# Multiplying the loaded gates two blocks at a time, one pair every second block

## The chip, the cores and the metric

The kernel runs on one NeuronCore of a Trainium2 chip. The metric is the device time of one execution in microseconds (us). TensorE is called PE here, VectorE DVE, ScalarE ACT, GpSimd POOL and SyncE SP; SPq and POOLq are the queues on which SP and POOL issue DMA.

## The reference, cut to what matters

The program is two transformer blocks on 256 tokens of width 2048. The change lies in the last part, a mixture of 16384 tiny experts ("PEER"):

```python
vals, ci = lax.top_k(cand, PEER_TOPK)          # 16 experts for each token and head
g = jax.nn.softmax(vals, axis=-1)              # their gates
...
u = u_table[it]
a = jnp.einsum('td,tkd->tk', ht, u)
w = jax.nn.gelu(a, approximate=False) * gt     # gt: the gates
return jnp.einsum('tk,tkd->td', w, v_table[it])
```

The kernel computes it densely: gelu of all 16384 expert activations, times a gate matrix G that is zero where a token did not choose the expert, times the whole table v.

## The kernel before, in words

The 16384 experts are 128 blocks of 128. Blocks 0 to 63 have their activations in the tile `bigA` ([128, 64, 256], one plane of 128 experts x 256 tokens for each block), blocks 64 to 127 in `bigB`.

- **Stage u** computes the activations, block by block (`u_block`): two weight chunks of 512 KB, 32 matmuls (L367, L370), then ACT copies one half of the result (L425), DVE adds the other (L427), and ACT takes the gelu (L1430). While blocks 0 to 63 run, DVE also selects the experts, and POOL scatters the gates to the matrices G0 and G1 in DRAM, one for each half of the tokens (L1412).
- **Stage v** multiplies with the table v, in four parts of 64 blocks: bigA for the first half of the output columns, bigA for the second, bigB for the second, bigB for the first. A block is one weight chunk of 512 KB and 12 matmuls (L1494 to L1496, four times), and `operands` prepares it.

Every weight chunk comes by DMA into one of 4 `raw` buffers. ACT rounds it to `wh` (L341, 3 buffers) and DVE forms the rest `wl` = raw - wh (L342, 2 buffers). So the `wl` of a chunk can be written only when PE is done with the chunk two before it, and PE's second matmul of a block needs it. The activations are split in the same way: ACT writes the rounded part into `xh` (L1487), DVE the rest (L1488), in a ring of 8 slots (`wxs`). That ring takes the memory of the input of stage u, so nothing is written to it before the last matmul of stage u.

The gate of a block must be multiplied into its plane before the block is split. Gates are loaded in pairs of blocks: `pair` is a [128, 2, 256] tile with 3 buffers, filled by two DMAs of POOL, from G0 and from G1 (L1472). `operands` asks for the pair of its block and the one after, and multiplies plane by plane on DVE (L1486).

A scheduler orders the instructions of each engine ahead of time; an engine then runs its list in order and stands at an instruction whose wait is not fulfilled. `tc.high_priority()` lets the weight splits pass other work. `tc.issue_after(x)` puts an instruction behind x in the list of its engine, and beyond that the scheduler is free. `self.added` is the last addition L427 that was written.

Of the kernel before, what the change touches and what calls it, by code (L numbers as in the profile page):

```python
# [11 lines left out]
F32 = mybir.dt.float32  # L12
# [4 lines left out]
OP = mybir.AluOpType  # L17
# [4 lines left out]
T = 256  # L22
# [164 lines left out]
class K:  # L187
# [871 lines left out]
    def block2(self):  # L1059
# [3 lines left out]
        with ExitStack() as cx:  # L1063
# [190 lines left out]
            TT, STT, TS = nc.vector.tensor_tensor, nc.vector.scalar_tensor_tensor, nc.vector.tensor_scalar  # L1254
            G, G2, GB, _, B, B2 = [ws[:, i:i + 1] for i in range(6)]
            with tc.issue_after(last.ins):
# [15 lines left out]
            TT(a, a, r, OP.mult)  # L1272
            TS(a, a, B, 1.0 / D, op0=OP.add, op1=OP.mult)
            TT(e, e, r, OP.mult)
# [36 lines left out]
    def peer(self, out):  # L1311
        nc, tc, a = self.nc, self.tc, self.a
        W = self.W
        xh = self.h2h
        with ExitStack() as cx:
# [3 lines left out]
            A = bigp.tile([128, 64, T], F32, name="bigA")  # L1319
# [15 lines left out]
            for g in range(4):  # L1335
                q = tk.tile([128, 4, T], F32, name="q", bufs=2)
# [89 lines left out]
            def u_block(b, dst):  # L1426
                def ev(ps):
                    t = self.tmp()
                    self.addh(t.unsqueeze(1), ps)
                    nc.scalar.activation(dst, t, AF.Gelu)  # L1430
                self.dense_t([a["u"][b, c] for c in range(2)], xh, ev, nt=1, kc=8, nw=128)
# [6 lines left out]
            tkc.close()  # L1438
            bigq = cx.enter_context(tc.tile_pool(name="bigB", bufs=1))
            B = bigq.tile([128, 64, T], F32, name="bigB")  # L1440
            for b in range(64):
                u_block(64 + b, B[:, b])
            self.drain()

            def final_rows(row, xs, xt, gt):
# [16 lines left out]
            acc = self.xhp.tile([128, 4, 1024], F32, name="xh")  # L1462
            wxs = self.xhp.tile([128, 8, 512], F32R, name="xh")

            pairs = {}

            def gates(q):

                if q < 64 and q not in pairs:
                    t = pairs[q] = sm.tile([128, 2, T], F32, name="pair", bufs=3)  # L1470
                    for tt in range(2):
                        nc.gpsimd.dma_start(t[:, :, tt * 128:tt * 128 + 128],  # L1472
                                            self.G[tt][:, q * 256:q * 256 + 256].rearrange("p (i t) -> p i t", i=2))
                return pairs.get(q)

            gated = set()

            def operands(big, dh, b):
                H, L = self.wchunk(self.vchunk(dh, b), 1, 1024)
                wx = wxs[:, b % 8]  # L1480
                if b not in gated:
                    gated.add(b)
                    g = gates(b // 2)
                    gates(b // 2 + 1)
                    with tc.issue_after(self.added.ins):
                        nc.vector.tensor_tensor(big[:, b % 64], big[:, b % 64], g[:, b % 2], OP.mult)  # L1486
                nc.scalar.copy(wx[:, :T], big[:, b % 64])  # L1487
                nc.vector.tensor_tensor(wx[:, T:], big[:, b % 64], wx[:, :T].bitcast(F32), OP.subtract)  # L1488
                return H, L, wx

            def product(o, tt, dc, ops, first, last):
# [8 lines left out]
            def part(ps, big, dh, b0, b1, first=False, last=False):  # L1500
                for b in range(b0, b1):
                    ops = operands(big, dh, b)
                    for tt, dc in four:
                        product(ps[tt][dc], tt, dc, ops, first and b == b0, last and b == b1 - 1)
                    self.pump()

            def banks():
                return [[self.bank() for dc in range(2)] for tt in range(2)]
# [30 lines left out]
            def first_half():  # L1539
                for tt, dc in four:  # L1540
                    add(tt, 0, dc, acc[:, tt, dc * 512:dc * 512 + 512])
                    yield

            self.tasks.append(final_rows(row, xs, xt, gt))
            self.tasks.append(first_half())
            part(ps, B, 1, 64, 128, False, True)
            self.drain()
# [3 lines left out]
            ps = banks()  # L1551
            part(ps, B, 0, 64, 125, True)
            ops = [operands(B, 0, b) for b in range(125, 128)]
            for tt in range(2):
                for dc in range(2):
# [47 lines left out]
```

## Time and profile before

| | |
|---|---|
| median of 3 runs | 3229.49 us (3226.41 to 3237.59) |
| the profiled execution | 3225.47 us, span of its trace 3223.7 us |
| PE busy | 3118.0 us (97% of the span) |
| DVE busy | 2381.3 us (74%) |
| ACT busy | 1738.8 us (54%) |
| POOL busy | 665.1 us (21%) |

Busy time is an average over the whole program. PE is close to full, so what there is to win are the stretches in which it stands or runs slowly, and these are read from the rows below, stage by stage. Stage u ends at about 2461 us of the span, stage v is the rest.

### The profile page before, as it was taken

What the parts mean: (1) busy time and instruction counts of PE and PEld (TensorE: products, weight loads), DVE (VectorE), ACT (ScalarE), POOL (GpSimd) and SP (SyncE); (2) the same over time, 40 slices, a digit from 0 to 9 for tenths busy, and PEclk for the clock granted to TensorE, in tenths of its full rate; (3) what the DMA queues carried; (4) which work ended last, traced back from release to release, by engine and by line L of the source; (5) the groups of instructions that cost most, each with busy time, mean ns of one, the idle gap of its engine ahead of it and who ended that gap; (6) DMA issues with size and microseconds to landing.
All of it is one profiled execution on the core that took longest, in us unless ns stands there. A gap on an engine that the chain in (4) does not pass through costs nothing.

```text
span 3223.7 us, 45942 instructions
## 1 busy us (share of the span) xinstructions
PE 3118.0 (97%) x16626; PEld 2671.7 (83%) x16626; DVE 2381.3 (74%) x3945; ACT 1738.8 (54%) x2632; POOL 665.1 (21%) x429
## 2 busy tenths in 40 slices
PE   8999899999999998999989999999999899999997
PEld 7888788888888887888878888888887678888886
DVE  6768889889999998668879985555556765555656
ACT  6676654444444576556665665455554345455453
POOL 0000000000000001000005778877862610000000
PEclk9999999999999998999989999999999999999999
DMA  6655589999999848555446776677676766565554
GB/s 236 206 177 185 170 280 328 331 335 325 330 327 332 304 162 333 177 174 166 148 146 164 183 184 190 190 190 190 190 201 215 253 210 194 192 228 196 191 194 150
DMA packets 235316, 715.55 MB, mean 222 GB/s; under 512 B 60512, under 2 KB 60896, under 8 KB 234448
## 3 DMA queue, kind: packets, MB, share of 16 engines
q1 hardware_dynamic: 185472, 671.97, 61.2%
q0 software_dynamic: 48176, 35.74, 6.4%
q10 hardware_dynamic: 1440, 4.91, 0.4%
q8 instruction: 130, 2.13, 0.3%
q14 instruction: 98, 0.80, 0.1%
HBM read 690.22 MB, written 21.11 MB: 221 GB/s over the span
## 4 chain that ended last, share of the span: by engine, by line
PE 78%; DVE 9%; DMA 2%; issue 1%; ACT 1%; POOL 0%; DVEq 0%; POOLq 0%; ACTq 0%
PE bank L367 37%; PE bank L370 19%; PE bank L1495 6%; PE bank L1494 6%; PE bank L1496 6%; DVE wl L342 3%; DMA pair<-G 2%; PE bank L412 1%; PE bank L413 1%; PE bank L414 1%; POOL pair L1472 0%; DVE t L1307 0%; PE bank L629 0%; ACT wh L341 0%; DVE sel L1378 0%
## 5 line engine op out<-in xcount | busy, mean ns | idle before, releaser
L342 DVE TENSOR_TENSOR wl<-raw,wh 128x1024 fp32r<-128x1024 f32 x1066 | 1302.1, 1222 | 717.4 <-PE bank L370 355.7
L367 PE MATMUL bank<-xh,wh 128*128 128x512 f32 x5264 | 1729.0, 396 | 37.3 <-DVE xh L455 20.5
L341 ACT CAST wh<-raw 128x1024 fp32r<-128x1024 f32 x1067 | 1119.2, 1050 | 846.3 <-PE bank L367 695.2
L370 PE MATMUL bank<-xh,wl 128*128 128x256 f32 x5264 | 1297.0, 282 | 0.3
L367 PEld LDWEIGHTS bank<-xh,wh 128*128 128x128 f32 x5264 | 980.1, 189 | 248.4 <-issue 19.4
L370 PEld LDWEIGHTS bank<-xh,wl 128*128 128x128 f32 x5264 | 930.9, 190 | 23.3 <-DVE wl L342 6.6
L1412 POOL DMA_INDIRECT G<-gate,at x256 | 550.3, 2150 | 183.6 <-DMA G<-gate,at 96.9
L1495 PE MATMUL bank<-wl,xh 128*128 128x512 f32 x1016 | 400.7, 394 | 24.7 <-DVE wl L342 24.5
L1494 PE MATMUL bank<-wh,xh 128*128 128x512 f32 x1020 | 400.8, 393 | 2.6 <-ACT xh L1487 2.6
L1496 PE MATMUL bank<-wh,xh 128*128 128x512 f32 x1020 | 399.5, 392 | 0.0
L1495 PEld LDWEIGHTS bank<-wl,xh 128*128 128x128 f32 x1016 | 192.2, 189 | 74.4 <-DVE wl L342 35.5
L1067 POOL DMA_DIRECT2D masks<-masks x1 | 0.7, 698 | 1218.6 <-DVE acc_z L472 1218.6
L771 DVE CUSTOM_DVE_ANT_0 raw<-raw,crow 128x1024 f32<-128x1024 f32 x192 | 234.0, 1219 | 15.4 <-DMA raw<-w_ada 15.3
L1494 PEld LDWEIGHTS bank<-wh,xh 128*128 128x128 f32 x1020 | 192.9, 189 | 43.4 <-ACT xh L1487 2.9
L1496 PEld LDWEIGHTS bank<-wh,xh 128*128 128x128 f32 x1020 | 193.0, 189 | 39.7
L367 PE MATMUL bank<-fx,wh 128*128 128x512 f32 x704 | 180.6, 393 | 0.0
L427 DVE TENSOR_TENSOR tmp<-bank,tmp 128x256 f32<-128x256 f32 x388 | 153.5, 419 | 11.0 <-ACT tmp L425 10.2
L1487 ACT CAST xh<-bigA 128x256 fp32r<-128x256 f32 x128 | 51.9, 408 | 198.2 <-PE bank L1495 194.3
L367 PEld LDWEIGHTS bank<-fx,wh 128*128 128x128 f32 x704 | 126.9, 189 | 23.4 <-DVE fx L903 0.2
L1487 ACT CAST xh<-bigB 128x256 fp32r<-128x256 f32 x128 | 52.3, 409 | 173.6 <-PE bank L1495 173.6
L425 ACT COPY tmp<-bank 128x256 f32<-128x256 f32 x388 | 132.1, 373 | 22.9 <-PE bank L370 22.2
L1472 POOL DMA_DIRECT2D pair<-G x128 | 91.2, 720 | 107.6 <-DVE bigA L1486 81.0
(405 smaller groups left out, 2353.7 us busy)
## 6 DMA issues: line engine op xcount, KB each, us to landing
raw<-u SPq DMA_DIRECT2D x256, 512.0 KB
raw<-v SPq DMA_DIRECT2D x256, 512.0 KB
raw<-w_ada SPq DMA_DIRECT2D x192, 512.0 KB
raw<-w_gu SPq DMA_DIRECT2D x176, 512.0 KB
raw<-w_in SPq DMA_DIRECT2D x144, 512.0 KB
raw<-w_down SPq DMA_DIRECT2D x88, 512.0 KB
raw<-w_out SPq DMA_DIRECT2D x32, 512.0 KB
raw<-w_ple_gate SPq DMA_DIRECT2D x32, 512.0 KB
```

The source lines that it names most:

```text
L341: nc.scalar.copy(H[:, :n], raw[:, :n])
L342: nc.vector.tensor_tensor(L[:, :n], raw[:, :n], H[:, :n].bitcast(F32), OP.subtract)
L367: self.nc.tensor.matmul(p, lhsT=H[:, kk, c], rhs=xh(k0 + kk), start=k0 + kk == 0, stop=False)
L370: self.nc.tensor.matmul(p[:, T:], lhsT=L[:, kk, c], rhs=xh(k0 + kk)[:, :T], start=False, stop=k0 + kk == nk - 1)
L425: self.nc.scalar.copy(out[:, j], p[:, T:])
L427: self.added = self.nc.vector.tensor_tensor(out[:, j], p[:, :T], out[:, j], OP.add)
L771: nc.vector.tensor_tensor_reduce(raw, raw, self.crow[:, h * 1024:h * 1024 + 1024], 1.0, 0.0, OP.mult, OP.add, s[:, h:h + 1])
L1412: nc.gpsimd.indirect_dma_start(out=self.G[tt].rearrange("p (f o) -> (p f) o", o=1), out_offset=bass.IndirectOffsetOnAxis(ap=places[tt, h][ ...
L1487: nc.scalar.copy(wx[:, :T], big[:, b % 64])
L1494: nc.tensor.matmul(o, lhsT=wH, rhs=H[:, 0, c], start=first, stop=False)
L1495: nc.tensor.matmul(o, lhsT=wH, rhs=L[:, 0, c], start=False, stop=False)
L1496: return nc.tensor.matmul(o, lhsT=wL, rhs=H[:, 0, c], start=False, stop=last)
```

## The change: what it does

The pairs are now numbered in the order of the blocks, P0 to P63, and two helpers work through them. `load_gates` starts the two DMAs of the next pair, and `apply_gates` starts one more load and multiplies the oldest loaded pair into its two planes, in one instruction of 128x512. It is called after each of the last five blocks of stage u (P0 to P4) and then in every second block of stage v, five pairs ahead of its use, so that P63 is multiplied in block 116 of the 256. In stage v `self.added` is now the split L1488 of the block just written, and so the multiplication stands behind that split in DVE's list; in stage u it is still the addition of the block.

```diff
+            loaded = deque()
+            blocks = deque(range(0, 128, 2))
+            def load_gates():
+                if blocks:
+                    b = blocks.popleft()
+                    t = sm.tile([128, 2, T], F32, name="pair", bufs=3)
+                    for tt in range(2):
+                        nc.gpsimd.dma_start(t[:, :, tt * 128:tt * 128 + 128],
+                                            self.G[tt][:, b * 128:b * 128 + 256].rearrange("p (i t) -> p i t", i=2))
+                    loaded.append((b, t))
+            def apply_gates():
+                load_gates()
+                if loaded:
+                    b, t = loaded.popleft()
+                    w = (A if b < 64 else B)[:, b % 64:b % 64 + 2]
+                    with tc.issue_after(self.added.ins):
+                        nc.vector.tensor_tensor(w, w, t, OP.mult)
             for b in range(64):
                 u_block(64 + b, B[:, b])
+                if b == 57:
+                    load_gates()
+                    load_gates()
+                if b >= 59:
+                    apply_gates()
...
             def operands(big, dh, b):
                 H, L = self.wchunk(self.vchunk(dh, b), 1, 1024)
                 wx = wxs[:, b % 8]
-                if b not in gated:
-                    gated.add(b)
-                    g = gates(b // 2)
-                    gates(b // 2 + 1)
-                    with tc.issue_after(self.added.ins):
-                        nc.vector.tensor_tensor(big[:, b % 64], big[:, b % 64], g[:, b % 2], OP.mult)
                 nc.scalar.copy(wx[:, :T], big[:, b % 64])
-                nc.vector.tensor_tensor(wx[:, T:], big[:, b % 64], wx[:, :T].bitcast(F32), OP.subtract)
+                self.added = nc.vector.tensor_tensor(wx[:, T:], big[:, b % 64], wx[:, :T].bitcast(F32), OP.subtract)
+                if b % 2 == 0:
+                    apply_gates()
                 return H, L, wx
```

How the lists move is shown at three places of DVE. Two are at the hand-over from stage u to stage v. Line numbers after the changed lines shift: L1486 (multiplication) becomes L1461, L1488 (split) L1496, L1472 (gate load) L1450. V0, V1, ... are the blocks of stage v.

DVE before, at the hand-over: `wl_23746` belongs to V1, `wl_23768` to V2, and the addition of `tmp_23787` is the last one of stage u.

```order
L427 TENSOR_TENSOR tmp_23738<-bank_23693,tmp_23738 128x256
L342 TENSOR_TENSOR wl_23719<-raw_23716,wh_23718 128x1024
L342 TENSOR_TENSOR wl_23746<-raw_23743,wh_23745 128x1024
L427 TENSOR_TENSOR tmp_23787<-bank_23742,tmp_23787 128x256
L1486 TENSOR_TENSOR bigA_15923<-bigA_15923,pair_23803 128x256 x2
L1486 TENSOR_TENSOR bigA_15923<-bigA_15923,pair_23806 128x256
L1488 TENSOR_TENSOR xh_23792<-bigA_15923,xh_23792 128x256 x3
L1486 TENSOR_TENSOR bigA_15923<-bigA_15923,pair_23806 128x256
L1486 TENSOR_TENSOR bigA_15923<-bigA_15923,pair_23851 128x256 x2
L1488 TENSOR_TENSOR xh_23792<-bigA_15923,xh_23792 128x256 x2
L342 TENSOR_TENSOR wl_23768<-raw_23765,wh_23767 128x1024
L1488 TENSOR_TENSOR xh_23792<-bigA_15923,xh_23792 128x256
```

DVE now, at the same place: `pair_23654` is P3, `pair_23760` P5, `pair_23813` P6, `pair_23707` P4; `wl_23737`, `wl_23768` and `wl_23790` belong to V0, V1 and V2, and `tmp_23809` is the last addition of stage u.

```order
L427 TENSOR_TENSOR tmp_23756<-bank_23711,tmp_23756 128x256
L1461 TENSOR_TENSOR bigA_15923<-bigA_15923,pair_23654 128x512
L342 TENSOR_TENSOR wl_23737<-raw_23734,wh_23736 128x1024
L1496 TENSOR_TENSOR xh_23818<-bigA_15923,xh_23818 128x256
L1461 TENSOR_TENSOR bigA_15923<-bigA_15923,pair_23760 128x512
L1496 TENSOR_TENSOR xh_23818<-bigA_15923,xh_23818 128x256 x2
L342 TENSOR_TENSOR wl_23768<-raw_23765,wh_23767 128x1024
L1461 TENSOR_TENSOR bigA_15923<-bigA_15923,pair_23813 128x512
L427 TENSOR_TENSOR tmp_23809<-bank_23764,tmp_23809 128x256
L1461 TENSOR_TENSOR bigA_15923<-bigA_15923,pair_23707 128x512
L342 TENSOR_TENSOR wl_23790<-raw_23787,wh_23789 128x1024
```

The first split of V0 no longer stands behind the last addition of stage u, multiplications have moved ahead into stage u, and P4 now comes behind P5, P6 and that last addition.

The rows right behind these, now: `pair_23831` is P7, `pair_23875` P8, and `wl_23826` and `wl_23850` belong to V3 and V4.

```order
L1496 TENSOR_TENSOR xh_23818<-bigA_15923,xh_23818 128x256 x2
L1461 TENSOR_TENSOR bigA_15923<-bigA_15923,pair_23831 128x512
L1496 TENSOR_TENSOR xh_23818<-bigA_15923,xh_23818 128x256
L342 TENSOR_TENSOR wl_23826<-raw_23823,wh_23825 128x1024
L1496 TENSOR_TENSOR xh_23818<-bigA_15923,xh_23818 128x256
L1461 TENSOR_TENSOR bigA_15923<-bigA_15923,pair_23875 128x512
L1496 TENSOR_TENSOR xh_23818<-bigA_15923,xh_23818 128x256 x2
L342 TENSOR_TENSOR wl_23850<-raw_23847,wh_23849 128x1024
```

Each of these `wl` stands behind the multiplication of another pair than before. With 3 buffers, P7 is loaded into the buffer that P4 leaves.

Further into stage v, DVE before has three or four multiplications for every block:

```order
L342 TENSOR_TENSOR wl_23917<-raw_23914,wh_23916 128x1024
L1488 TENSOR_TENSOR xh_23792<-bigA_15923,xh_23792 128x256
L1486 TENSOR_TENSOR bigA_15923<-bigA_15923,pair_24301 128x256
L1486 TENSOR_TENSOR bigA_15923<-bigA_15923,pair_24346 128x256 x2
L342 TENSOR_TENSOR wl_23938<-raw_23935,wh_23937 128x1024
L1488 TENSOR_TENSOR xh_23792<-bigA_15923,xh_23792 128x256
L1486 TENSOR_TENSOR bigA_15923<-bigA_15923,pair_24391 128x256 x2
L1486 TENSOR_TENSOR bigA_15923<-bigA_15923,pair_24436 128x256 x2
```

DVE now, further into stage v:

```order
L1496 TENSOR_TENSOR xh_23818<-bigA_15923,xh_23818 128x256
L1461 TENSOR_TENSOR bigA_15923<-bigA_15923,pair_24007 128x512
L342 TENSOR_TENSOR wl_23914<-raw_23911,wh_23913 128x1024
L1496 TENSOR_TENSOR xh_23818<-bigA_15923,xh_23818 128x256
L342 TENSOR_TENSOR wl_23938<-raw_23935,wh_23937 128x1024
L1496 TENSOR_TENSOR xh_23818<-bigA_15923,xh_23818 128x256
```

One multiplication stands in the list for every two blocks, behind a split, and this pattern lasts until P63.

## Rows read from the trace of the kernel before

**Rows 1.** Stretches: length, busy PE, PEld, DVE, ACT, POOL; granted clock, DMA share, GB/s.

```profile
2300.00:2400.00 100.00, 100.00 (x579) 88.17 (x578) 51.69 (x54) 50.30 (x72) 79.31 (x37) 1.00 0.71 194
2463.00:2605.00 142.00, 116.36 (x454) 87.60 (x455) 102.96 (x210) 53.59 (x83) 86.37 (x122) 0.95 0.78 249
2605.00:2825.00 220.00, 219.92 (x971) 181.78 (x970) 127.67 (x164) 112.04 (x166) 0.00 (x0) 1.00 0.60 195
```

**Rows 2.** Waits from 2461 to 2606 us: total, times, longest.

```profile
PE bank L1495 <- DVE wl L342: 24.5, 21, 2.4
...
DVE bigB L1486 <- DMA pair<-G: 22.1, 16, 2.5
DVE bigA L1486 <- DMA pair<-G: 16.6, 19, 1.8
...
PE bank L1494 <- ACT xh L1487: 2.6, 1, 2.6
```

**Rows 3.** PE in order of time: the end of stage u, the start of stage v.

```profile
2461.22 0.28 PE L370 MATMUL bank<-xh,wl 128*128 128x256 f32 x1
2464.06 0.50 PE L1494 MATMUL bank<-wh,xh 128*128 128x512 f32 x1 [2.56 <-ACT xh L1487]
```

**Rows 4.** DVE in order of time, just after the last gate multiplication.

```profile
2608.72 1.23 DVE L342 TENSOR_TENSOR wl<-raw,wh 128x1024 fp32r<-128x1024 f32 x1 [0.90 <-issue]
```

**Rows 5.** Groups of DVE from 2458.7 to 2608 us.

```profile
L342 DVE TENSOR_TENSOR wl<-raw,wh 128x1024 fp32r<-128x1024 f32 x40 | 48.8, 1219 | 2.7 <-PE bank L370 2.7
L1486 DVE TENSOR_TENSOR bigB<-bigB,pair 128x256 f32<-128x256 f32 x64 | 24.6, 421 | 22.2 <-DMA pair<-G 22.1
L1486 DVE TENSOR_TENSOR bigA<-bigA,pair 128x256 f32<-128x256 f32 x64 | 24.6, 421 | 16.8 <-DMA pair<-G 16.6
```

**Rows 6.** The nearest group to a multiplication of 128x512 on DVE.

```profile
L1534 DVE TENSOR_TENSOR bigA<-bigA,xh 128x512 f32<-128x512 f32 x12 | 8.2, 680 | 0.1
```

**Rows 7.** DVE in order of time, the last blocks of stage u.

```profile
2457.27 0.42 DVE L427 TENSOR_TENSOR tmp<-bank,tmp 128x256 f32<-128x256 f32 x1
2458.77 1.23 DVE L342 TENSOR_TENSOR wl<-raw,wh 128x1024 fp32r<-128x1024 f32 x1 [1.07 <-PE bank L370]
2461.60 1.23 DVE L342 TENSOR_TENSOR wl<-raw,wh 128x1024 fp32r<-128x1024 f32 x1 [1.60 <-PE bank L370]
```

**Rows 8.** One block of stage v without gates, all engines in order of time.

```profile
2654.90 0.41 ACT L1487 CAST xh<-bigA 128x256 fp32r<-128x256 f32 x1 [1.36 <-PE bank L1495]
2654.93 0.39 PE L1494 MATMUL bank<-wh,xh 128*128 128x512 f32 x1
...
2654.96 1.23 DVE L342 TENSOR_TENSOR wl<-raw,wh 128x1024 fp32r<-128x1024 f32 x1 [1.16 <-issue]
...
2656.10 0.42 DVE L1488 TENSOR_TENSOR xh<-bigA,xh 128x256 fp32r<-128x256 f32 x1
...
2657.65 0.39 PE L1494 MATMUL bank<-wh,xh 128*128 128x512 f32 x1
...
2657.88 0.39 PE L1495 MATMUL bank<-wl,xh 128*128 128x512 f32 x1
```

**Rows 9.** The chain that ended last, from a freed gate buffer to its load landed.

```profile
2478.07 0.28 issue
2478.36 0.71 POOL pair L1472
2479.07 4.56 DMA pair<-G
...
2506.34 0.28 issue
...
2508.74 5.46 DMA pair<-G
```

**Rows 10.** Size of a gate load, two of which make a pair.

```profile
pair<-G POOLq DMA_DIRECT2D x128, 128.0 KB
```

**Rows 11.** A stretch with one fall of the granted clock, columns as in Rows 1.

```profile
2500.00:2520.00 20.00, 15.38 (x57) 11.62 (x58) 13.94 (x28) 6.35 (x9) 12.18 (x18) 0.91 0.79 251
```

More of the change, by code (lines that the diff above doesn't have):

```diff
@@ L1463, in peer @@
             wxs = self.xhp.tile([128, 8, 512], F32R, name="xh")
[L1465 to L1476, printed above, removed]
             def operands(big, dh, b):
```

## The prediction

> **What bounds the kernel now.** I read the busy time by stretches first. In stage u (2300 to 2400 us) and in the later stage v (2605 to 2825) PE is busy all the time at clock 1.00, and nothing can be won there. In between, from 2463 to 2605 us, PE is busy for 116 of 142 us at a mean clock of 0.95, while DVE is busy for 103 us and POOL issues gate loads [rows 1]. The view of the waits says who holds whom: PE waits 24.5 us for `wl` from DVE, and DVE stands 22.1 + 16.6 = 38.7 us for gate loads to land [rows 2]. So this stretch is paced by the gate loads: all 128 multiplications are in it [rows 5], DVE stands in front of them, and the `wl` behind them in its list come late to PE. Ahead of it PE stands once for 2.56 us, until the first block of stage v is multiplied and split [rows 3].
>
> What the stretch costs is counted in blocks. Undisturbed, a block of stage v takes 2.72 us (its first product at 2654.93, that of the next at 2657.65 [rows 8]). A `wl` begins just after the first product of the block ahead of its own (2654.96 against 2654.93 [rows 8]). Forty `wl` lie between 2458.7 and 2608 us [rows 5], V0 to V39, so that of 2608.72 is V40's [rows 4], and V39 began on PE at 2608.7. Stage u ended at 2461.22 + 0.28 = 2461.5 [rows 3]. With no loss V39 would have begun at 2461.5 + 39 x 2.72 = 2567.6. The gates cost **41.1 us**: 24.5 + 2.6 us of waiting, 0.05 x 142 = 7.1 us of granted clock, and the rest slow starts after each wait.
>
> **The change, part by part.**
>
> *Wider multiplications.* 128 of 421 ns [rows 5] become 64 of about 680 ns [rows 6]: 53.9 - 43.5 = 10 us less on DVE. By itself worth nothing where DVE has room.
>
> *The even pace.* In stage v each two blocks (5.44 us) now hold two `wl`, two splits and one multiplication: 2 x 1.22 + 2 x 0.42 + 0.68 = 3.96 us of DVE, 73%. The multiplication falls into the 1.16 us in which DVE stands idle between a split and the next `wl` [rows 8]. If it came late there, `wl` ends 1.23 us after its start at 2654.96 and its product comes only at 2657.88 [rows 8], 1.7 us later. So it is hidden, with 0.5 us of idle time and 1.7 us of slack as cover; without the cover it would cost 0.68 us x 59 pairs = 40 us, all of the gain.
>
> *The loads.* In the chain a buffer freed at 2478.07 is filled and landed at 2483.63, 5.6 us later (0.28 until POOL, 0.71 for its issue, 4.56 for the DMA); with other loads ahead of it on POOL, from 2506.34 to 2514.2, 7.9 us [rows 9]. Three buffers give each load up to 2 x 5.44 us, so in the steady part no wait is left. A pair is 256 KB [rows 10], so the traffic is about 262 / 5.44 = 48 GB/s on top of 195, or 243 GB/s; in the gate stretch 249 flowed, and stage u runs with PE full at a DMA share of 0.71 [rows 1].
>
> *The hand-over* is where a cost remains, and I walk it through in the order of DVE's new list, with the times of before [rows 7]. The addition of the last but one block of stage u ends at 2457.7, P3 at 2458.4, `wl` of V0 runs from 2458.8 to 2460.0. ACT may write into the ring only at 2461.5 and needs 0.41 us [rows 8], so V0 begins on PE at about 2462.1 instead of 2464.06; the second split comes at 2462.4. Then P5 to 2463.0, two splits to 2463.8, `wl` of V1 to 2464.9 (needed at 2465.2). P6 was loaded into the buffer that P3 left at 2458.4, landed at about 2464: no wait, done 2465.6. The last addition 2466.0, P4 2466.6, `wl` of V2 2467.8 (needed 2467.9), two splits 2468.5. Now P7: its buffer is that of P4, free at 2466.6, landed at 2466.6 + 5.2 = 2471.8 (5.6 in the chain, less where the DMA queues are emptier). **DVE stands 3.3 us at P7**, and behind it in the list are a split and the `wl` of V3: 2471.8 + 0.65 + 0.35 + 1.22 = 2474.0. PE needs it at 2470.6 and waits 3.4 us. The `wl` of V4 then ends at 2476.9 (needed 2476.8), that of V5 at 2480.0 (needed 2479.6), and from V6 on DVE is ahead. The sum is 0.6 + 0.2 (the second split) + 3.4 + 0.1 + 0.4 = 4.7 us.
>
> Its bounds: with the slow 7.9 us of the chain for each load, P6 is late as well, and the waits are about 0.9 + 1.0 + 6.0 + 0.2 + 2.5 = 10.6 us; if every load landed in time, only the 0.8 us of the start would be left. P7 finds POOL idle, as the load of 5.6 us did, so I stay at 5.2.
>
> A gap of 3.4 us in PE's work may also lower its clock. A stretch with one fall has a mean of 0.91 over 20 us, a loss of 1.8 us, after waits that were none longer than 2.4 us [rows 2, 11]. I take 1 us (bounds 0 and two falls, 3.6). [...]
>
> [...]
>
> *The sum.* 41.1 - 4.7 - 1 = 35.4 us less: 3225.47 (span 3223.7 and 1.8 around it) - 35.4 = 3190.1. The profiled execution is below all three timed runs, whose median is 4.0 us higher; with part of that, I predict **3193**.
>
> **Rivals.**
>
> 1. *The hand-over is dear* (waits of 10.6 us and two falls of the clock, 14 in all): gain 27, about 3198 to 3203. For it: loads of 7.9 us in the chain [rows 9], and in the new list P7 and P8 are issued one after the other. Against: POOL is otherwise idle there. Chance 0.17.
> 2. [...] Chance 0.12.
> 3. *The waiting moves along*: DVE stands at each pair for its load, as it does now [rows 2]. It decides once loads take more than some 11 us; for a wait of PE of 0.3 us at each of 59 pairs the gain shrinks by 18 us, to about 3211. Against: 5.6 and 7.9 us [rows 9]. Chance 0.06.
> 4. *Slower*: the gate loads share the DMA engines with the weights for some 110 blocks of PE instead of 40, and the weights come late. Each block would have to take 0.32 us longer (2.72 to 3.04) to eat 35 us, and 0.41 to lose 0.3%, about 3239. For it: 243 GB/s against 195 now. Against: 249 in the gate stretch, and PE's waits there are for DVE, not for a weight load [rows 1, 2]. Chance 0.04.
> 5. *No change*: PE could be slow in the stretch for a reason that stays when the multiplications leave. Against: 2605 us, where the last multiplication is done and the clock and PE are full at once [rows 1, 4]. Chance 0.03.
>
> **How the numbers follow.** The forecast (3188 to 3198) has a chance of 0.58. A measurement tells 0.3%, 9.7 us, from no change. The forecast, rivals 1 and 2, and most of rival 3 are faster by more: 0.92; same 0.04; slower 0.04. The range 3184 to 3206 takes in rivals 1 and 2, and leaves out 3 to 5, with some room for the 4 us between the profiled and the median run.
>
> **What would show it.** In the profile after: PE's waits for `wl` after 2461 us fall from 24.5 us to some 4, in one gap near V3, and DVE's waits for gate loads from 38.7 to some 3 or 4, nearly all at P7; V0 begins about 0.6 us after the end of stage u; the last gate multiplication (P63, in block 116, whose split is written when its ring slot 8 blocks before is free) stands near 2466 + 109 x 2.72 = 2762 us, and blocks take 2.72 us throughout; the granted clock falls once or not at all. I am wrong if `wl` is late by a little at many pairs (the cover of 1.16 us is then not there), if DVE stands at pairs far into stage v, or if blocks before 2762 us take longer than those behind with DVE idle (then it is the weights).

## The result, and the profile after

The changed kernel takes 3197.32 us (median of 4 runs, 3195.54 to 3202.18), beside 3233.54 us for the kernel before on the same chip: a ratio of 0.9892, 95% interval 0.9868 to 0.9917. In the second comparison (5 runs, below) it was 0.9873, 0.9854 to 0.9892. So the change makes the kernel 1.1 to 1.3% faster, some 36 to 41 us.

The profiled execution took 3202.18 us, and its span, 3200.4 us, is only 23.3 us shorter than that of before. A block of stage u takes 5.545 us in some executions and 5.655 us in others, of either kernel, so that the times of each kernel fall into two clusters some 10 us apart. The kernel before was profiled in a short one and the changed kernel in a long one. The count of matmuls in 100 us of stage u tells which it was, 579 in [rows 1] and 569 here. The view by stretches of the changed kernel (length, busy PE, PEld, DVE, ACT, POOL; granted clock, DMA share, GB/s):

```profile
2300.00:2400.00 100.00, 100.00 (x569) 86.70 (x568) 51.01 (x54) 49.83 (x72) 84.25 (x38) 1.00 0.67 191
2463.00:2605.00 142.00, 140.18 (x628) 116.03 (x627) 98.52 (x137) 71.24 (x111) 41.76 (x60) 0.99 0.76 243
2605.00:2700.00 95.00, 95.00 (x421) 78.67 (x420) 64.72 (x88) 49.27 (x75) 24.72 (x35) 1.00 0.76 241
```

The second row answers to the gate stretch of [rows 1], though its first 13 us are here still the end of stage u, at 2475.75: PE is busy for 140.2 of 142 us, where it was 116.4, and its clock is 0.99 instead of 0.95. From 2605 us the multiplications still run (DVE has 64.7 us to do), and PE is not held up by them.

The waits of the changed kernel from 2461 to 2700 us (total, times, longest), in place of [rows 2]:

```profile
DVE bigA L1461 <- DMA pair<-G: 3.3, 1, 3.3
...
PE bank L1505 <- DVE wl L342: 1.8, 1, 1.8
```

Of PE's 24.5 us in 21 waits one of 1.8 us is left, and of DVE's 38.7 us for gate loads one of 3.3 us. Where it comes from is in the chain that ended last (start, length, what) and, behind it, in DVE's and PE's rows in order of time:

```profile
2471.75 0.69 DVE bigA L1461
2472.44 0.28 issue
...
2473.43 6.92 DMA pair<-G
```

```profile
2480.44 0.69 DVE L1461 TENSOR_TENSOR bigA<-bigA,pair 128x512 f32<-128x512 f32 x1 [3.33 <-DMA pair<-G]
...
2483.25 0.50 PE L1505 MATMUL bank<-wl,xh 128*128 128x512 f32 x1 [1.82 <-DVE wl L342]
...
2483.87 0.63 PE L1504 MATMUL bank<-wh,xh 128*128 128x512 f32 x1
2484.30 0.63 PE L1505 MATMUL bank<-wl,xh 128*128 128x512 f32 x1
```

P3 is done at 2472.44 and frees the buffer of P6. The load lands some 7.9 us later, DVE stands 3.3 us at P6, and behind it are the last addition of stage u, P4 and the `wl` of V2. PE waits 1.8 us for that `wl`, and from 2483.87 us its products start 0.43 us apart instead of 0.23: the granted clock is 0.50 from 2483.8 to 2487 us. From 2480 to 2500 us its mean is 0.91:

```profile
2480.00:2500.00 20.00, 18.18 (x74) 14.54 (x73) 16.93 (x28) 9.72 (x15) 9.89 (x14) 0.91 0.77 252
```

That is 0.09 x 20 = 1.8 us more, in one fall behind a wait of 1.82 us. A wait of such a length does not always bring a fall: the run without early multiplications (below) has waits of 2.83 and 1.30 us, and its granted clock is 1.00 in every stretch from 2461 to 2520 us. So 3.6 of the 41.1 us are left in this execution, all of it at the hand-over.

The start of stage v costs nothing at all. PE's first product follows the last matmul of stage u without a gap, where [rows 3] had 2.56 us, because ACT had begun to write the ring 1.9 us before stage u ended (ACT's row, six writes together, stands first):

```profile
2473.83 1.94 ACT L1495 CAST xh<-bigA 128x256 fp32r<-128x256 f32 x6
...
2475.47 0.28 PE L370 MATMUL bank<-xh,wl 128*128 128x256 f32 x1
2475.58 0.40 PE L1504 MATMUL bank<-wh,xh 128*128 128x512 f32 x1
```

Further into stage v DVE's rows show the pace. The multiplication lies between a split and the next `wl`, which then has 0.56 us of idle time before it, and 1.16 us in the blocks without one ([rows 8]); a `wl` starts every 2.72 us:

```profile
2656.19 1.22 DVE L342 TENSOR_TENSOR wl<-raw,wh 128x1024 fp32r<-128x1024 f32 x1 [1.16 <-ACT xh L1523]
2657.33 0.42 DVE L1496 TENSOR_TENSOR xh<-bigA,xh 128x256 fp32r<-128x256 f32 x1
2657.67 0.69 DVE L1461 TENSOR_TENSOR bigB<-bigB,pair 128x512 f32<-128x512 f32 x1
2658.91 1.23 DVE L342 TENSOR_TENSOR wl<-raw,wh 128x1024 fp32r<-128x1024 f32 x1 [0.56 <-issue]
```

### The profile page after: what moved, and what is told of

Same layout as the page of the kernel before. It is cut to its first block, busy times and chain, and to the rows that moved or that the text cites. A ratio compares the mean times of both kernels' runs of the same rounds, so it can differ in the third digit from the quotient of the medians.

```text
span 3200.4 us, 45877 instructions
## 1 busy us (share of the span) xinstructions
PE 3119.2 (97%) x16626; PEld 2673.7 (84%) x16626; DVE 2375.7 (74%) x3881; ACT 1737.6 (54%) x2632; POOL 690.7 (22%) x429
## 4 chain that ended last, share of the span: by engine, by line
PE 92%; DVE 5%; ACT 1%; DMA 1%; issue 1%; DVEq 0%; POOL 0%; ACTq 0%; SPq 0%
PE bank L367 43%; PE bank L370 22%; PE bank L1505 7%; PE bank L1506 7%; PE bank L1504 7%; DVE wl L342 1%; PE bank L412 1%; PE bank L413 1%; PE bank L414 1%; PE bank L658 0%; PE bank L629 0%; ACT wh L341 0%; DMA raw<-w_ada 0%; PE bank L1189 0%; DMA raw<-w_in 0%
## 5 line engine op out<-in xcount | busy, mean ns | idle before, releaser
L1412 POOL DMA_INDIRECT G<-gate,at x256 | 576.0, 2250 | 161.1 <-DMA G<-gate,at 61.8
L427 DVE TENSOR_TENSOR tmp<-bank,tmp 128x256 f32<-128x256 f32 x388 | 153.2, 419 | 10.8 <-ACT tmp L425 10.2
L1450 POOL DMA_DIRECT2D pair<-G x128 | 91.1, 719 | 264.2 <-DVE bigA L1461 144.7
```

The costliest lines, as they stand in the source:

```text
L427: self.added = self.nc.vector.tensor_tensor(out[:, j], p[:, :T], out[:, j], OP.add)
L1412: nc.gpsimd.indirect_dma_start(out=self.G[tt].rearrange("p (f o) -> (p f) o", o=1), out_offset=bass.IndirectOffsetOnAxis(ap=places[tt, h][ ...
```

## The experiments

In the expectations two times stand for the two lengths of stage u's blocks, and so they do in what was measured: the median of the runs in the shorter cluster, then in the longer. For the kernel before these are 3228.7 and 3238.4 us (25 and 45 runs over all comparisons), for the changed kernel 3186.2 and 3196.7 us (4 and 10 runs). Like for like the change is worth 42.5 and 41.7 us. Which cluster a run belongs to was read from the trace for each profiled execution; the other runs are put there by their times. A second measure leaves stage u out: from the end of its last matmul to the end of the span it is 762.2 and 761.3 us in the two profiles of the kernel before, and 724.7, 721.3 and 721.1 us in the three of the changed kernel. By it the change is worth 37 to 41 us; this time is called stage v's below.

**The two kernels again.** Both unedited, on one chip.

> The changed kernel once more, unedited, to see which of its differences from the kernel before come back. Theory: stage v keeps what it gained (first product of stage v to last product some 37 us shorter than before, one wait for wl of about 1.8 us near V2, DVE standing once for about 3.3 us at P6), and the 2% longer blocks in the second half of stage u (5.655 against 5.545 us) vary from execution to execution, whatever the kernel; then this profile may show 5.545 or 5.655. Rival: the longer blocks of stage u belong to the change (its other program, its other placement of weights or code); then they are here again at 5.65, and not in the run of the kernel before. Median near 3197 by both.

> The kernel before once more, unedited. Theory: 3226 to 3238 us, with 24 to 25 us of waits for wl in the gate stretch; the blocks of stage u at 5.545 or 5.655 us as the execution falls, and where the profile is the longer one (some 3235 us), the 10 us are in stage u. Rival: 5.545 in every execution of this kernel, and its spread of 3226 to 3238 has another place.

The changed kernel took 3195.15 us, ratio 0.9873 (0.9854 to 0.9892); the kernel before against itself gave 0.9994 (0.998 to 1.0008). Now the lengths of stage u are the other way round: the changed kernel was profiled in a short execution (first two rows), the kernel before in a long one (third row).

```profile
2300.00:2400.00 100.00, 100.00 (x578) 88.17 (x578) 51.84 (x55) 50.34 (x73) 82.95 (x38) 1.00 0.67 194
2463.00:2605.00 142.00, 141.84 (x626) 117.15 (x625) 101.11 (x140) 71.99 (x109) 42.80 (x62) 1.00 0.77 250
```

```profile
2300.00:2400.00 100.00, 100.00 (x568) 86.76 (x567) 50.07 (x53) 49.01 (x71) 84.58 (x36) 1.00 0.65 187
```

So the longer blocks are no work of the change: my theory held and the rival fell. In the kernel before PE waits 26.4 us for `wl` (2461 to 2720 us), a little more than the 24 to 25 I had given. What held only in part is the hand-over: I had expected its wait of 3.3 us at P6 to come back. Here DVE stands 0.6 us, at P7 (and once more later), and PE is busy for 141.84 of 142 us.

```profile
DVE bigA L1461 <- DMA pair<-G: 1.2, 2, 0.6
...
PE bank L1505 <- DVE wl L342: 0.2, 1, 0.2
```

**The width alone.** In the kernel before:

```diff
-                    gated.add(b)
+                    gated.update((b, b + 1))
...
-                        nc.vector.tensor_tensor(big[:, b % 64], big[:, b % 64], g[:, b % 2], OP.mult)
+                        nc.vector.tensor_tensor(big[:, b % 64:b % 64 + 2], big[:, b % 64:b % 64 + 2], g, OP.mult)
```

> The kernel before with one part of the change alone: two planes are multiplied in one instruction of 128x512, and everything else stays (no multiplication during stage u, no pace). Theory (loads that land late in front of wl are what costs): DVE has some 10 us less to do in the stretch but waits for loads that much longer, since 64 pairs still pass through 3 buffers; PE's waits for wl stay at 18 to 26 us, and the time is that of before within 0.3%, 3224 to 3240. Rival (DVE's own work paces the stretch, 103 us for 38 blocks of 2.72 us): some 10 us of the 41 are gone, about 3223.

Ratio 0.9976 (0.9964 to 0.9989); 3219.5 and 3230.5, so 9 and 8 us less. The ratio is within the 0.3% I gave, but the gain is real (runs of 3218 us lie below my range, which began at 3224), and its size is the rival's. Its waits from 2461 to 2606 us for gate loads, and then for `wl` (2461 to 2720 us):

```profile
DVE bigA L1486 <- DMA pair<-G: 16.5, 17, 2.9
DVE bigB L1486 <- DMA pair<-G: 14.1, 21, 1.9
```

```profile
PE bank L1495 <- DVE wl L342: 19.6, 26, 2.2
```

DVE still stands 30.6 us and PE 19.6 us (38.7 and 24.5 in [rows 2]); I had expected DVE to wait some 10 us longer, and it waits 8 us less. The clock falls less too (a mean of 0.99 instead of 0.95 from 2463 to 2605 us). I take it that less work shortens what comes behind each wait, which no run shows by itself. Most of the loss stays.

**No pace.** The changed kernel, in which the multiplications of stage v are no longer held behind a split:

```diff
-                self.added = nc.vector.tensor_tensor(wx[:, T:], big[:, b % 64], wx[:, :T].bitcast(F32), OP.subtract)
+                nc.vector.tensor_tensor(wx[:, T:], big[:, b % 64], wx[:, :T].bitcast(F32), OP.subtract)
```

> The changed kernel without the pace: in stage v the multiplication stands behind the last addition of stage u alone, so that in DVE's list the multiplications move ahead, one to two in each block, and are over after some 40 to 60 blocks instead of 116. The wide multiplications and the five during stage u stay. Theory (a pair needs 5.6 to 7.9 us from free to landed, and 3 buffers give it only 3 to 5 us at this rate, with a wl behind each): DVE stands at many pairs again, PE waits 10 to 25 us for wl, about 3207 to 3225. Rival (the width and the early ones are the gain, the pace is not): 3197 as with the pace.

Ratio 0.9961 (0.9948 to 0.9974); 3216.6 and 3226.7, so 30 us slower than the changed kernel. The last pair is multiplied by 2585 us, and the waits from 2461 to 2720 us are nearly those of before:

```profile
PE bank L1505 <- DVE wl L342: 22.5, 21, 2.4
...
DVE bigB L1461 <- DMA pair<-G: 17.7, 19, 2.1
...
DVE bigA L1461 <- DMA pair<-G: 15.0, 13, 3.5
```

As the theory had it: 30 of the 42 us are the pace, and the width and the early ones without it bring 12. By stage v's time (753.0 us) it is 32 of 41, and 9.

**Narrow, paced.** The changed kernel with two multiplications of 128x256 for a pair:

```diff
-                        nc.vector.tensor_tensor(w, w, t, OP.mult)
+                        for i in range(2):
+                            nc.vector.tensor_tensor(w[:, i], w[:, i], t[:, i], OP.mult)
```

> The changed kernel with the pair multiplied in two instructions of 128x256 again, and the pace and the early ones kept. Theory (paced, the multiplication lies in DVE's idle time between a split and the next wl, 1.16 us, and two of 0.42 us still fit): the same time as the changed kernel within 0.3%, 3186 to 3189 in the executions whose stage u takes 5.545 us a block, 3196 to 3202 in those of 5.655. Rival (the width counts by itself: it took some 8 us off the kernel before): 64 x (2 x 0.42 - 0.68) = 10 us slower, 3196 and 3206.

3185.9 and 3196.6: the same as the changed kernel. The width that brought 8 us to the kernel before brings nothing here, since the multiplication lies in DVE's idle time (from 2605 to 2700 us DVE is busy for 65.9 of 95 us, PE for all of them).

**None early.** The changed kernel with P0 to P4 written after stage u:

```diff
-                if b == 57:
-                    load_gates()
-                    load_gates()
-                if b >= 59:
-                    apply_gates()
             self.drain()
+            for i in range(2):
+                load_gates()
+            for i in range(5):
+                apply_gates()
```

> The changed kernel without multiplications during stage u: the same two loads and five calls, but written after stage u's last block, so that P0 to P6 stand behind the last addition in DVE's list; the pace of stage v stays. Theory (what the early ones save is the landing of loads at the hand-over, with 3 buffers for seven pairs wanted at once): V0 begins 1 to 2.6 us late, and DVE stands at P3 to P8 for loads, in all 6 to 12 us more than the changed kernel, with falls of the clock: 3193 to 3200 and 3203 to 3212. Rival (they only move 3.4 us of DVE's work, and the ring of splits makes it up): at most 3 us more, 3189 and 3199.

3193.1 and 3203.8, 7 us slower than the changed kernel. V0 begins late by the same wait for its split as in [rows 3]; DVE stands 3.1 us in four waits for gates, and PE waits 1.5 us for two `wl`:

```profile
DVE bigA L1461 <- DMA pair<-G: 3.1, 4, 1.5
...
PE bank L1503 <- ACT xh L1494: 2.8, 1, 2.8
...
PE bank L1504 <- DVE wl L342: 1.5, 2, 1.3
```

From 2480 to 2500 us PE begins 78 products instead of 90, at a clock of 1.00, which is 2.7 us: four of its products begin 0.2 to 1.5 us late, each on the `wl` of a chunk, and each time the next follows after 0.33 us instead of 0.23.

```profile
2480.00:2500.00 20.00, 18.37 (x78) 13.85 (x77) 16.39 (x26) 8.86 (x14) 14.57 (x22) 1.00 0.81 248
```

With the 2.8 us at the start this makes 5.5 us, and stage v's time (727.0 us) is 5.7 to 5.9 us above the better two of the changed kernel. The total, 7 us, is within my theory, but without a fall of the clock, and the landing of loads is only about half of it, the start of V0 the other half.

**Loads or DVE's work?** The kernel before, with one pair of gates loaded and used for every block:

```diff
-                    g = gates(b // 2)
-                    gates(b // 2 + 1)
+                    g = gates(0)
```

> The kernel before with a single pair of gates loaded and used for all 128 multiplications: it leaves out all loads of gates but one, and multiplies every block with the gates of the first two. Three theories of the 41 us that the gates cost before. Loads alone: DVE never stands, all but the 2.6 us of the start is won, 3189 and 3199. DVE's work alone: nothing changes, 3227 and 3237. Mine: both; without the loads DVE still has 1.22 + 0.42 + 3.4 x 0.42 = 3.1 us for each block of 2.72 us while the multiplications last, some 0.4 x 38 = 15 us, and the 2.6 us of the start, so that some 18 us of the 41 stay: 3204 and 3214.

3192.1 (one run) and 3199.2: 37 to 39 us less than before. That is the theory of the loads alone, and mine was wrong. Stage v's time is 723.7 us, 2.6 more than the best of the changed kernel. DVE is busy without a break, and PE misses nothing but the start, which is these 2.6 us (a stretch, and the one wait of PE that is left):

```profile
2520.00:2560.00 40.00, 40.00 (x179) 33.10 (x178) 40.00 (x87) 19.81 (x30) 0.00 (x0) 1.00 0.56 186
```

```profile
PE bank L1493 <- ACT xh L1486: 2.6, 1, 2.6
```

A DVE at 100% does not hold up PE here. It is not that the multiplications make way: three or four of them stand between two `wl`, as in the kernel before. A block of four, in DVE's rows:

```profile
2502.33 1.22 DVE L342 TENSOR_TENSOR wl<-raw,wh 128x1024 fp32r<-128x1024 f32 x1
2503.47 0.42 DVE L1487 TENSOR_TENSOR xh<-bigA,xh 128x256 fp32r<-128x256 f32 x1
2503.80 1.43 DVE L1485 TENSOR_TENSOR bigA<-bigA,pair 128x256 f32<-128x256 f32 x4
2505.14 1.22 DVE L342 TENSOR_TENSOR wl<-raw,wh 128x1024 fp32r<-128x1024 f32 x1
```

In these rows an instruction starts before the time of the one ahead is over: behind a `wl` of 1.22 us the split starts after 1.14, and four multiplications of 0.42 us take 1.34. Such a block takes DVE 2.81 us, one of three multiplications 2.48, and from 2480.38 to 2570.97 us a `wl` starts every 2.75 us on average. Beside PE's 2.72 that is 0.8 us too much over 33 blocks, which the slack of `wl` takes up. My 3.1 us had added up the durations as though they did not overlap.

**The pace from V6 on.** The changed kernel without a multiplication in V0, V2 and V4, where the ring of eight splits fills and asks for pairs in a burst:

```diff
-                if b % 2 == 0:
+                if b % 2 == 0 and (big is B or dh or b >= 6):
```

> The changed kernel without a multiplication in V0, V2 and V4, so that the pairs, five ahead of their use, are no longer asked for in a burst while the ring of eight splits fills. Theory (in the first profile after the change P6 came in 7.7 us after its buffer was free and cost PE 1.8 us and a fall of the clock, in the second it came in less than 4.5 us and cost nothing): the wait cannot occur any more, PE waits under 0.5 us for wl after 2461, and the time is that of the changed kernel or up to 3.6 us less; the executions spread less within each of the two lengths of stage u. Rival (any pair can land late and wl then waits for it, wherever it stands): waits of 1 to 3 us turn up at other pairs, and the time is the same.

3186.7 and 3196.1, not to be told from the changed kernel. Its profile shows neither a wait of PE for `wl` nor one of DVE for gates after 2461 us, and the clock is 1.00 in every stretch from 2461 to 2700 us. The wait at P6 does not occur in this profile, but nor does it in two of the three profiles of the changed kernel, so that one profile does not show that it is gone, and this many runs don't show a gain.

**Two buffers.** The changed kernel with `bufs=2` for `pair` and one load ahead instead of two:

```diff
-                    load_gates()
                     load_gates()
...
-                    t = sm.tile([128, 2, T], F32, name="pair", bufs=3)
+                    t = sm.tile([128, 2, T], F32, name="pair", bufs=2)
```

> The changed kernel with 2 buffers for the pairs instead of 3 (and one load ahead of the first multiplication instead of two): a load then has one period of 5.44 us less the multiplication, 4.8 us from free to wanted, where it has 10.2 us in the changed kernel. The multiplication itself may come some 2.2 us late (0.5 us of idle time and 1.7 us of slack) before wl is missed. Theory (loads of 5.6 to 7.9 us, as in the chain of the kernel before, need the third buffer): DVE stands 1 to 3 us at most of the 59 pairs, PE up to 1 us at a part of them, 10 to 40 us slower than the changed kernel, 3197 to 3227. Rival (at the steady pace loads land faster than in the chain, in under 5 us, so the third buffer is for the hand-over alone): DVE stands under 0.5 us a pair, PE hardly ever, and the time is within 5 us of the changed kernel, in both lengths of stage u.

3199.5 us, all five runs in the longer cluster: 3 us slower than the changed kernel. The rival was right about the time. DVE stands 5.7 us in six waits, all before 2493 us, and from 2500 us on never; the loads of the steady part (issues from 2520 to 2700 us: KB, median us from issue to landing) take 4.3 us:

```profile
pair<-G POOLq DMA_DIRECT2D x66, 128.0 KB, 4.3
```

The run does not test whether loads land within the 4.8 us that I had given them. A buffer is wanted again two pairs later with two buffers and three pairs later with three. The last load, that of P63, waits for P61 here (the first three rows) and for P60 in the changed kernel (the last three):

```profile
2762.31 0.69 DVE L1461 TENSOR_TENSOR bigB<-bigB,pair 128x512 f32<-128x512 f32 x1
2763.30 1.41 POOL L1450 DMA_DIRECT2D pair<-G  x2 [4.04 <-DVE bigB L1461]
2773.19 0.69 DVE L1461 TENSOR_TENSOR bigB<-bigB,pair 128x512 f32<-128x512 f32 x1
```

```profile
2761.03 0.69 DVE L1461 TENSOR_TENSOR bigB<-bigB,pair 128x512 f32<-128x512 f32 x1
2762.01 1.41 POOL L1450 DMA_DIRECT2D pair<-G  x2 [4.03 <-DVE bigB L1461]
2777.35 0.68 DVE L1461 TENSOR_TENSOR bigB<-bigB,pair 128x512 f32<-128x512 f32 x1
```

From free to wanted it is 10.2 us with two buffers and 15.6 with three. So even the slow load of 7.9 us [rows 9] would have had room with two, and the third buffer and the second load ahead serve the hand-over only.

**More traffic.** The changed kernel with a copy of the same size, from G to a spare place in DRAM, beside each gate load:

```diff
                         nc.gpsimd.dma_start(t[:, :, tt * 128:tt * 128 + 128],
                                             self.G[tt][:, b * 128:b * 128 + 256].rearrange("p (i t) -> p i t", i=2))
+                        nc.gpsimd.dma_start(spare[tt][:, b * 128:b * 128 + 256],
+                                            self.G[tt][:, b * 128:b * 128 + 256])
```

> The changed kernel with a second DMA of the same size and queue beside each gate load, from G to a spare place in DRAM that nobody reads: POOL issues twice as many, 2.8 us of each 5.44, and some 48 GB/s come on top of 243. Theory (a pair has 10.2 us from free to wanted, PE's weights come with room): loads land in 7 to 10 us, PE keeps its 2.72 us a block, and the time is that of the changed kernel within 0.3%, apart from 0 to 6 us at the hand-over. Rival (the DMA queues were near their limit, so that weights or gates come late): blocks of over 2.8 us until the last pair, 9 us or more slower.

3215 to 3242 us, and it says nothing on its question. The copies wait for no buffer, so the scheduler put them all ahead of the gate loads in POOL's list, but for those of the first three pairs; the other loads came only when the copies were done, and DVE stood for one of them for 44.5 us:

```profile
2476.78 16.50 POOL L1453 DMA_DIRECT2D spare<-G  x32 [0.30 <-DMA spare<-G]
...
2494.66 16.14 POOL L1453 DMA_DIRECT2D spare<-G  x31 [0.18 <-issue]
2510.79 4.26 POOL L1451 DMA_DIRECT2D pair<-G  x6
```

So each copy was tied behind its own load:

```diff
-                        nc.gpsimd.dma_start(t[:, :, tt * 128:tt * 128 + 128],
+                        d = nc.gpsimd.dma_start(t[:, :, tt * 128:tt * 128 + 128],
...
+                        with tc.issue_after(d.ins):
+                            nc.gpsimd.dma_start(spare[tt][:, b * 128:b * 128 + 256],
+                                                self.G[tt][:, b * 128:b * 128 + 256])
```

> The changed kernel with the spare copies once more, each now placed right behind its own gate load in POOL's list, so that they come at the pace of the loads: POOL issues some 2.5 us in each 5.44, and some 48 GB/s come on top of 241 until P63. Theory (weights and gates have room at the even pace): PE stays at 100% and 2.72 us a block from 2520 to 2700 us, DVE does not stand at a pair there, and the time is that of the changed kernel within 0.3%, apart from 0 to 10 us at the hand-over, where the burst of loads has the copies between them: 3184 to 3197 and 3195 to 3207. Rival (weights near their limit): PE waits for weights or wl in the steady part and blocks take over 2.8 us, 3200 or more in the executions with the shorter stage u.

3190.3 and 3201.0, 4 us slower, and the 4 us are at the hand-over (three waits of PE for `wl`, 3.1 us in all, and a fall of the clock, to a mean of 0.91 from 2480 to 2500 us). In the steady part PE loses nothing at a DMA share of 0.88 and 291 GB/s, against 0.76 and 241 in the changed kernel:

```profile
2605.00:2700.00 95.00, 95.00 (x421) 78.73 (x420) 64.69 (x87) 49.45 (x74) 43.58 (x69) 1.00 0.88 291
```

**The changed kernel a third time.**

> The changed kernel a third time, unedited, beside the two others on the same chip. Theory: two clusters again, near 3186 and 3197, by the length of stage u's blocks; at the hand-over PE's wait for wl is anything from 0 to 2 us, as the load of P6 falls. Rival: the waits at the hand-over go with the length of stage u (5.655: wait; 5.545: none).

3195.2 us; 3184.5 and 3186.8, then 3195.2 to 3197.2. The profile is of a long execution and PE waits for no `wl` at all after 2461 us; DVE stands once for 1.0 us, at P7, the last of these rows (P5, POOL's next load, P4, P7):

```profile
2471.63 0.68 DVE L1461 TENSOR_TENSOR bigA<-bigA,pair 128x512 f32<-128x512 f32 x1
2472.61 1.42 POOL L1450 DMA_DIRECT2D pair<-G  x2 [1.45 <-DVE bigA L1461]
...
2474.97 0.68 DVE L1461 TENSOR_TENSOR bigA<-bigA,pair 128x512 f32<-128x512 f32 x1
...
2478.47 0.69 DVE L1461 TENSOR_TENSOR bigA<-bigA,pair 128x512 f32<-128x512 f32 x1 [1.01 <-DMA pair<-G]
```

So the wait at the hand-over does not go with the length of stage u, and of three profiles it cost PE 1.8, 0.2 and 0 us.

## Why the prediction was right, and where it was not

**What bounds.** The reading held: the loads that DVE stood at, with `wl` behind them, cost the stretch. With the loads taken away and all of DVE's work kept, 37 to 39 us go; with the work made shorter and the loads kept, 8 to 9. The 41.1 us counted there are a good measure: 41.7 and 42.5 were won, like for like, and stage v's best time, 721.1 us, is 41.1 below that of the profile of before.

**Wider multiplications.** "By itself worth nothing where DVE has room" is right for the paced list (0 us) and gave no price for the list of before, where it is worth 8 to 9 us: there DVE is nearly always busy or waiting (103 and 38.7 us in a stretch of 142).

**The even pace and the loads.** Both held. The multiplication takes 0.69 us in the 1.16 us of idle time, no steady wait is left, and P63 stands at 2777.35 us, which is 2763 counted from an end of stage u 14.25 us earlier, as in the profile of before (2762 was the forecast). Two terms were too cautious. "Three buffers give each load up to 2 x 5.44 us" is one period short: it is 15.6 us, and rival 3 would have needed loads as slow as that. And DVE's 3.96 us for two blocks add up durations that overlap: it is busy for 64.7 of 95 us, 68% and not 73%, and 0.56 us of idle time are left behind a multiplication. [rows 5] had shown it, since 64 multiplications of 421 ns are busy for 24.6 us and not 26.9. What the loss of the idle time would cost was priced too high as well: the run with one pair has DVE full at 2.75 us a block without a loss, so the "0.68 us x 59 pairs = 40 us" would not have followed.

**The hand-over** is the term that was mis-sized: "4.7 us" of waits and 1 us of clock, where the three profiles show PE waiting 1.8, 0.2 and 0 us, and one fall of the clock, 1.8 us, in the first alone. Three steps in it failed. "ACT may write into the ring only at 2461.5" (and the words ahead of the prediction that nothing is written to it before stage u's last matmul) is wrong: ACT wrote it 1.9 us ahead of stage u's end, and the 0.8 us at the start did not arise. In the kernel stage u's input is two tiles of eight slices each, and the ring takes the memory of one of them, so that it need not wait for all; what released it, the trace does not show. "Its buffer is that of P4" (said of P7 ahead of the prediction too) is wrong as well. The loads follow one another in DVE's order of multiplications, and P5 is multiplied before P4: in the third profile POOL issues the load at 2472.61, when P5 is done and P4 has not begun. So P7 goes into P5's buffer, 3.3 us earlier; in place of 3.3 us DVE stood at P7 for 0, 0.6 and 1.0 us. That P7's load would take less where the queues are emptier (5.2 us for 5.6) was an estimate; in the steady part a gate DMA takes 4.3 us at 241 GB/s in all (two buffers) and 5.1 at 290 (the tied copies). And the walk gave P6 "no wait", which held in two profiles, while in the first its load took 7.9 us from free to landed, as the slow one of the chain of before [rows 9] did, and held up DVE for 3.3 us. That this is the number that I had forecast is chance: it is another pair, and another reason. So a nearly free hand-over, rival 2 with its 0.12, is the more usual case, with PE waiting 0.2 and 0 us in two of the three profiles. Loads much quicker than before are not shown as the reason: in the third profile the gate DMAs issued from 2465 to 2490 us took 4.4 us from issue to landing (median of 20), and the chain of before has 4.56 and 5.46 [rows 9]. Why the load of P6 takes under 5 us in one execution and 7.9 in another stays open; with pairs asked for later no wait was left in the one profile taken.

**The median.** For a profiled execution with the shorter stage u the sum gave 3190.1 us; these runs took 3186.2, some 4 us less, since the hand-over cost hardly anything. I then added 3 us for the distance of profile and median. Measured, the clusters lie 10 us apart, and 10 of 14 runs of the changed kernel are in the longer one, so the median came out at 3195 to 3197. The two errors, 4 us too dear and 7 us too little, go against each other, so that the median lies within the range of the forecast, 3188 to 3198, partly by luck; the gain itself does not rest on it.

**The other rivals.** The weights have room (291 GB/s without a loss), the waiting did not move along, and the stretch had no other reason to be slow.

## What to carry to other kernels

When an engine stands in a fixed list, look at what is queued behind the instruction that waits, not only at how full the engine is: DVE at 100% cost PE nothing, as its work for a block (2.75 us) was hardly longer than PE's, and DVE at 73% with 39 us of waits for loads cost it 41. Side work that needs loads is best bound to the pace of the main work by an order (one for every two blocks), a few ahead; without the bond the scheduler pulled it into a burst here. With the bond the width of the instruction did not matter. Durations of one engine's rows can overlap (DVE's split began 1.14 us after the start of a `wl` of 1.22), so its work is better taken from start to start than added up. And before a difference of some 10 us is explained, both kernels should be profiled twice.

## What was not expected of the hardware

Stage u has two speeds with the clock at 1.00 and PE at 100% in both. Within an execution all its blocks keep one of them from the 28th on. In the kernel before, PE's rows in a short and in a long execution:

```profile
2300.14 0.39 PE L367 MATMUL bank<-xh,wh 128*128 128x512 f32 x1
...
2300.49 0.39 PE L367 MATMUL bank<-xh,wh 128*128 128x512 f32 x1
```

```profile
2300.08 0.40 PE L367 MATMUL bank<-xh,wh 128*128 128x512 f32 x1
...
2300.44 0.40 PE L367 MATMUL bank<-xh,wh 128*128 128x512 f32 x1
```

A pair of matmuls takes 0.35 us in the one and 0.36 in the other by these rounded rows; over the 16 pairs of a block it is 5.545 against 5.655 us, or 0.347 against 0.353 a pair. Stage v takes 2.72 us a block in both. What decides between them is not known.
